# A two-layer hybrid decoder on one core: the order of two bank drains at the middle of a down unit, and where on-chip buffers begin

## The chip, the core and the metric

The kernel runs on one core of a Trainium2 chip. TensorE multiplies out of the on-chip memory (SBUF) into eight accumulation banks (PSUM), each 128 partitions by 512 float32 numbers; VectorE (DVE in the profile) and ScalarE (ACT) do the elementwise work and read the banks; SyncE (SP) issues the loads from HBM. The metric is the device time of one execution in microseconds. Three executions of the kernel before took 2243.55, 2243.8 and 2245.27 us, with a median of 2243.8 us.

## What is computed

Two layers on 256 tokens of width 2048, all in float32. Each layer has a mixing half (gated linear attention and stick-breaking attention side by side, one input and one output projection) and a squared-ReLU MLP with 8192 hidden columns. The change touches the end of the MLP in its order of work, and all of the kernel in where its buffers lie.

```python
D_MODEL, SEQ, DEPTH, D_FF = 2048, 256, 2, 4 * 2048

def hybrid_layer(x, ...):
    h = rms_norm(x, attn_norm)
    proj = h @ w_in                       # 2048 x 6160
    ...                                   # both head groups, from slices of proj
    x = x + mixed @ w_o                   # 2048 x 2048
    hm = rms_norm(x, mlp_norm)
    up = square(relu(hm @ w_up))          # 2048 x 8192
    return x + up @ w_down                # 8192 x 2048
```

## The kernel before

**Split products.** Every operand of the large products is held in the type `float32r` as two tiles, a high part and the remainder, called the low part, and each product is made of three: high times high, high times low, low times high. Weights come from HBM into a tile `raw`; ScalarE copies it to `whi` (the high part), VectorE subtracts to `wlo` (L358 and L360 for the projections, L990 and L991 for the down product). There are four buffers of `whi` and four of `wlo`, three of `raw`. Activations lie in 19 buffers of one size, `act`, high and low parts side by side.

**Three kinds of stage.** The projections are *units* (L365): weights move through TensorE, activations stay in the array as the stationary operand, 512 columns a product (L377 to L379). The up product and a part of the projections use the transposed form (`unit_t`, L411): activations move, weights are stationary, and a product of 512 columns (L424) is followed by one of 256 (L428). The down product (`mlp_down`, L961) is the third kind.

**A down unit.** The hidden columns are taken in four quarters a layer; for each quarter four `mlp_up` calls make 16 column blocks of `up`, and one down unit multiplies them with their 2048 rows of `w_down` and adds the result to the residual `xb`. So there are eight down units, four a layer. A unit goes through 16 `pairs` (L966), numbered `x`: the left 1024 output columns are x 0 to 7, the right 1024 are x 8 to 15; x takes 256 rows of `w_down`, one megabyte. For an even `j = x % 8`, and for j = 7, the block is multiplied plainly in two steps, `left` and `right` (L1071, L1076), 12 products each. For j = 1, 3 and 5 a scheme with sums of blocks saves products: seven block products instead of eight, in four steps (L1061). It needs sums of weight blocks, made by VectorE in `first` (L1037: the sums `ts`, then two more additions), and sums of activation blocks, made once during the up stage into tiles `sx` (L947). The first of the four steps is 6 products, the second 3, the third and fourth 6 each.

**The banks.** A half of a unit accumulates in eight banks, m1 to m8. When a half is done, its banks are added to `xb` by VectorE: m1, m5, m6, m7 after the last step of j = 5 (`drain`, L1049), m2 and m4 after `left` of j = 7 (`drain_left`, L1081), m3 and m8 after `right` of j = 7 (`drain_right`, L1087). The next half takes the same eight banks again (`new_banks`, L1006), so its first product into a bank waits for that bank's drain.

**The order.** In a down unit the instructions of TensorE, VectorE and ScalarE stand in the order in which the code records them. Each step has a part that prepares weights (`prepare`: splits and block sums, recorded at once) and a part with its products (`emit`, L1101: products, then the drain if the step has one). Steps go through a queue: when four are in it, the oldest is emitted. So the weights of a step are prepared three steps ahead of its products:

```python
for prepare, products, follow in steps(x):
    queue.append((x, products, prepare(), follow))
    if len(queue) >= LEAD:          # LEAD = 4
        emit(*queue.pop(0))
```

At the middle of a unit this gives the following order. Recording the preparation of x = 8 `right` emits x = 7 `left` with its drains of m2 and m4. Recording the first step of x = 9 (j = 1: the block sums) comes next, and only after it is x = 7 `right` emitted, with its drains of m3 and m8. "The second half" below means x 8 to 15, and "step 9a" to "step 9d" the four steps of x = 9.

**Buffers.** Pools are laid out in SBUF one after the other in the order in which they are opened (L67 to L72): constants, residual, activations, weights (`raw`, `whi`, `wlo`), temporaries, statistics, and then the pool of the attention or the MLP half (with `sx`, `ts`, `raw2`), which is reopened in turn.

Of the kernel before, what the change touches and what calls it, by code (L numbers as in the profile page):

```python
# [10 lines left out]
F32R = mybir.dt.float32r  # L11
# [5 lines left out]
P = 128  # L17
# [22 lines left out]
def trunk_kernel(  # L40
# [22 lines left out]
    def nm(s):  # L63
        uid[0] += 1
        return f"{s}_{uid[0]}"

    cpool = ctx.enter_context(tc.tile_pool(name="const", bufs=1))  # L67
    xpool = ctx.enter_context(tc.tile_pool(name="resid", bufs=1))
    apool = ctx.enter_context(tc.tile_pool(name="acts", bufs=19))
    wpool = ctx.enter_context(tc.tile_pool(name="weights", bufs=3))  # L70
    tpool = ctx.enter_context(tc.tile_pool(name="temps", bufs=2))
    spool = ctx.enter_context(tc.tile_pool(name="stats", bufs=6))  # L72

    pools = {}
    scopes = {}
# [44 lines left out]
    def f32(ap):  # L120
        return ap.bitcast(F32)
# [218 lines left out]
    def weight_parts(w2d, r0, c0, kt, width, fine=False, halves=1, order=lambda k: None):  # L340

        full = 2048 // kt
        raw = wpool.tile([P, kt, full], F32, tag="raw", name=nm("raw"))
        src = w2d[r0 : r0 + kt * P, c0 : c0 + width].rearrange("(k p) n -> p k n", p=P)
        step = 1 if fine else kt // halves
        for s in range(0, kt, step):
            nc.sync.dma_start(raw[:, s : s + step, :width], src[:, s : s + step, :])
        for s in range(2):
            hk = kt // 2
            hi = wpool.tile([P, hk, full], F32R, tag="whi", name=nm("whi"), bufs=4)  # L350
            lo = wpool.tile([P, hk, full], F32R, tag="wlo", name=nm("wlo"), bufs=4)
            step = 1 if fine else hk
            for q in range(0, hk, step):
                r = raw[:, s * hk + q : s * hk + q + step, :width]
                h = hi[:, q : q + step, :width]
                dep = order(s * hk + q)
                with tc.issue_after(dep) if dep else nullcontext():
                    newest["hi"] = nc.scalar.activation(h, r, AF.Copy).ins  # L358
                with tc.issue_after(st["first"]) if fine else nullcontext():
                    newest["lo"] = nc.vector.tensor_tensor(  # L360
                        lo[:, q : q + step, :width], r, f32(h), ALU.subtract
                    ).ins
            yield hi, lo

    def unit(op, w2d, row0, c0, width, groups=(0, 1, 2, 3), hooks={}, fine=0, split=False, order=lambda i, k: None):  # L365
# [17 lines left out]
        def prep(i):  # L383
            return weight_parts(
                w2d, row0 + 4 * groups[i] * P, c0, 4, width, fine=i < fine,
                halves=2 if fine else 1, order=lambda k: order(i, k),
            )
# [216 lines left out]
    for l in range(DEPTH):  # L604
# [356 lines left out]
        def mlp_down(q):  # L961
# [8 lines left out]
            def load(x):  # L970
                if x >= len(pairs):
                    return
                n2, j = pairs[x]
                if x % 5 < 2:
                    r = tmp("raw2", [P, 2, 1024], bufs=2)
                else:
                    r = wpool.tile([P, 2, 1024], F32, tag="raw", name=nm("raw"))
                raws[x] = r
                r0 = (q * KT + 2 * j) * P
                nc.sync.dma_start(  # L980
                    r,
                    w_down[l][r0 : r0 + 2 * P, n2 * 1024 : (n2 + 1) * 1024].rearrange(
                        "(k p) n -> p k n", p=P
                    ),
                )

            def parts(r, n=2):
                hi = wpool.tile([P, 2, 512], F32R, tag="whi", name=nm("whi"), bufs=4)
                lo = wpool.tile([P, 2, 512], F32R, tag="wlo", name=nm("wlo"), bufs=4)
                nc.scalar.activation(hi[:, :n], r, AF.Copy)  # L990
                nc.vector.tensor_tensor(lo[:, :n], r, f32(hi[:, :n]), ALU.subtract)  # L991
                return hi, lo
# [13 lines left out]
            def new_banks():  # L1006
                begun.clear()
                for m in (5, 1, 6, 7, 2, 4, 3, 8):
                    banks[m] = pools["m"].tile([P, 512], F32, tag=f"m{m}", name=nm(f"m{m}_"))

            def steps(x):
# [21 lines left out]
                if fast(j):  # L1033
# [3 lines left out]
                    def first():  # L1037
                        t13 = sums["t13"] = tmp("ts", [P, 2, 512], bufs=2)
                        t4 = sums["t4"] = tmp("t4", [P, 512], bufs=1)
                        b12 = r[:, 0, 512:]  # L1040
                        ends = r.rearrange("p k (c n) -> p (k c) n", c=2)[:, ::3, :]
                        nc.vector.tensor_tensor(  # L1042
                            t13, ends, b12.unsqueeze(1).to_broadcast([P, 2, 512]), ALU.add
                        )
                        add(b12, t13[:, 0, :], r[:, 1, 512:])
                        add(t4, b12, r[:, 1, :512])
                        return parts(r[:, 1, :].rearrange("p (c n) -> p c n", c=2))

                    def drain():  # L1049
# [11 lines left out]
                    return (  # L1061
                        (first, lambda w: (mm(2, blk(1, 0), w, 0, False), mm(3, ext(1), w, 1, False)), None),
                        (lambda: parts(sums["t4"].unsqueeze(1), 1), lambda w: mm(4, blk(1, 1), w, 0, False), None),
                        (lambda: parts(sums["t13"]),
                         lambda w: (mm(5, blk(0, 1), w, 0, lastf), mm(7, ext(2), w, 1, lastf)), None),
                        (lambda: parts(r[:, 0, :].rearrange("p (c n) -> p c n", c=2)),
# [32 lines left out]
            queue = []  # L1099

            def emit(x, products, w, follow):  # L1101
                if x % 8 == 0 and products.__name__ == "left":
                    new_banks()
                products(w)
                if follow:
                    follow()
# [2 lines left out]
                load(x)  # L1109
            for x in range(len(pairs)):  # L1110
                load(x + 4)
                for prepare, products, follow in steps(x):
                    queue.append((x, products, prepare(), follow))
                    if len(queue) >= LEAD:
                        emit(*queue.pop(0))
# [7 lines left out]
        for q in range(4):  # L1123
            if q:
                att_psum()
            for g in range(4):
                mlp_up(q, g)
            down_psum()
            with tc.manual_schedule(engines=MANUAL):
                mlp_down(q)  # L1130
# [40 lines left out]
```

## Time and profile before

| | before |
|---|---|
| median of three executions | 2243.8 us (2243.55 to 2245.27) |
| the profiled execution | 2244.34 us |
| its span, first to last instruction | 2242.6 us |
| TensorE busy | 2219.7 us |
| VectorE, ScalarE, GpSimd busy | 1628.6, 1171.0, 39.1 us |
| moved by DMA | 409.05 MB, 182 GB/s over the span |
| a down unit (the first, 508.5 to 594.2 us) | 85.7 us, TensorE busy 83.9, VectorE 75.5, ScalarE 45.3 |

The span is 1.7 us shorter than the profiled execution, which has its start and end around it. A matmul's duration in the profile runs to a modelled end and overlaps the next one's, so the time that a matmul costs is read as the distance from its start to the next one's start. "Idle" of an engine is counted from the end of its last instruction, and therefore is shorter than the gap between two starts. PE is TensorE, and PEld its weight load, which runs during the matmul before.

### The profile page before, as it was taken

The page shows a single profiled execution, that of the slowest core. Times are in us where ns is not written, and L with a number is a line of the kernel's source. Part 1 is how long each engine was busy: PE and PEld are TensorE (multiplying, and loading weights), DVE is VectorE, ACT ScalarE, POOL GpSimd, SP SyncE. Part 2 cuts the span into 40 slices and gives each one's busy share as a digit, 9 for nine tenths or more (in the row PEclk, how much of TensorE's full clock was granted, in tenths as well). Part 3 has the DMA queues.
Part 4 walks back from the last instruction along what each step waited for, and adds up shares of the span by engine and source line. Part 5 has one row for each costly group of instructions (what it writes and reads, how often), then busy time and mean ns, then how long its engine had stood idle before and what let it go on. Part 6 is the DMA issues. An engine that isn't in the chain of part 4 may idle for free.

```text
span 2242.6 us, 28461 instructions
## 1 busy us (share of the span) xinstructions
PE 2219.7 (99%) x11292; PEld 1858.6 (83%) x11292; DVE 1628.6 (73%) x2024; ACT 1171.0 (52%) x1499; POOL 39.1 (2%) x68
## 2 busy tenths in 40 slices
PE   9999999999999999999999999999999999999998
PEld 7988778887888888788788887888878878887887
DVE  5777565668868868867967775656787688688688
ACT  5555354555555455455555553555555545554553
POOL 0020000000000000000000200000000000000000
PEclk9999999999999999999999999999999999999999
DMA  6545446664665665565446544466656656656653
GB/s 228 189 158 162 151 144 232 187 188 169 214 186 188 201 188 187 190 195 179 169 135 204 171 151 150 154 225 184 188 183 203 187 178 207 188 181 210 185 180 127
DMA packets 250857, 409.05 MB, mean 182 GB/s; under 512 B 6650, under 2 KB 162882, under 8 KB 250724
## 3 DMA queue, kind: packets, MB, share of 16 engines
q1 hardware_dynamic: 250724, 407.24, 55.7%
q8 instruction: 88, 1.44, 0.3%
q14 instruction: 45, 0.37, 0.0%
HBM read 405.12 MB, written 2.10 MB: 182 GB/s over the span
## 4 chain that ended last, share of the span: by engine, by line
PE 91%; DVE 7%; issue 1%; ACT 1%; DMA 0%; POOL 0%; SPq 0%; POOLq 0%
PE acc L424 24%; PE acc L428 12%; PE acc L377 9%; PE acc L378 9%; PE acc L379 9%; DVE wlo L991 3%; DVE xb L1004 2%; DVE t L1004 1%; PE ps L294 1%; PE ps L847 1%; PE ps L859 1%; DVE ts L1042 0%; PE ps L806 0%; ACT whi L990 0%; PE ps L540 0%
## 5 line engine op out<-in xcount | busy, mean ns | idle before, releaser
L360 DVE TENSOR_TENSOR wlo<-raw,whi 128x1024 fp32r<-128x1024 f32 (+2 forms) x530 | 630.5, 1194 | 420.0 <-ACT whi L358 418.9
L358 ACT ACTIVATE whi<-raw 128x1024 fp32r<-128x1024 f32 (+2 forms) x530 | 545.3, 1032 | 643.9 <-PE acc L424 340.0
L424 PE MATMUL acc<-act,whi 128*128 128x512 f32 x2304 | 816.0, 399 | 0.0
L428 PE MATMUL acc<-act,wlo 128*128 128x256 f32 x2304 | 646.8, 281 | 0.0
L424 PEld LDWEIGHTS acc<-act,whi 128*128 128x128 f32 x2304 | 433.0, 188 | 106.5
L428 PEld LDWEIGHTS acc<-act,wlo 128*128 128x128 f32 x2304 | 435.2, 189 | 0.4
L377 PE MATMUL acc<-whi,act 128*128 128x512 f32 (+2 forms) x960 | 368.4, 384 | 0.5 <-ACT act L302 0.5
L378 PE MATMUL acc<-wlo,act 128*128 128x512 f32 (+2 forms) x960 | 361.9, 377 | 0.4 <-DVE wlo L360 0.4
L379 PE MATMUL acc<-whi,act 128*128 128x512 f32 (+2 forms) x960 | 361.6, 377 | 0.0
L991 DVE TENSOR_TENSOR wlo<-raw,whi 128x1024 fp32r<-128x1024 f32 x256 | 306.2, 1222 | 70.0 <-ACT whi L990 65.6
L990 ACT ACTIVATE whi<-raw 128x1024 fp32r<-128x1024 f32 x256 | 266.2, 1058 | 157.3 <-PE acc L424 29.0
L377 PEld LDWEIGHTS acc<-whi,act 128*128 128x128 f32 x960 | 180.9, 188 | 35.5 <-issue 4.1
L379 PEld LDWEIGHTS acc<-whi,act 128*128 128x128 f32 x960 | 180.5, 188 | 33.8 <-issue 0.7
L378 PEld LDWEIGHTS acc<-wlo,act 128*128 128x128 f32 x960 | 180.8, 188 | 32.0 <-DVE wlo L360 1.0
L990 ACT ACTIVATE whi<-t 128x512 fp32r<-128x512 f32 x48 | 30.4, 634 | 145.5 <-DVE t L1004 93.3
L991 DVE TENSOR_TENSOR wlo<-ts,whi 128x1024 fp32r<-128x1024 f32 x48 | 58.8, 1225 | 2.3 <-ACT whi L990 2.3
L1042 DVE TENSOR_TENSOR ts<-raw 128x1024 f32<-128x1024 f32 x48 | 58.5, 1218 | 0.0
L939 DVE TENSOR_TENSOR act<-t,act 128x512 fp32r<-128x512 f32 x64 | 44.1, 690 | 10.9 <-ACT act L938 10.9
L990 ACT ACTIVATE whi<-ts 128x1024 fp32r<-128x1024 f32 x48 | 50.2, 1045 | 0.0
L439 DVE TENSOR_TENSOR t<-acc,t 128x512 f32<-128x512 f32 x72 | 49.3, 684 | 0.0
L934 ACT ACTIVATE t<-t 128x512 f32<-128x512 f32 x64 | 39.6, 618 | 12.8 <-DVE t L930 12.8
L930 DVE SCALAR_TENSOR_TENSOR t<-t,row 128x512 f32<-128x512 f32 x64 | 44.3, 692 | 2.2
(1160 smaller groups left out, 2768.2 us busy)
## 6 DMA issues: line engine op xcount, KB each, us to landing
raw<-in_w_down_dram SPq DMA_DIRECT2D x128, 1024.0 KB, 5.3
raw<-in_w_up_dram SPq DMA_DIRECT2D x128, 1024.0 KB, 5.8
raw<-in_w_in_dram SPq DMA_DIRECT2D x84, 1024.0 KB, 5.1
raw<-in_w_o_dram SPq DMA_DIRECT2D x32, 1024.0 KB, 5.0
raw<-in_w_in_dram SPq DMA_DIRECT2D x14, 512.0 KB, 6.8
raw<-in_w_in_dram SPq DMA_DIRECT2D x8, 544.0 KB, 3.7
out_dram<-xb SPq DMA_DIRECT2D x8, 256.0 KB, 2.2
xb<-in_x_dram SPq DMA_DIRECT2D x3, 512.0 KB, 7.5
```

Of the source, the lines that this page charges most:

```text
L358: newest["hi"] = nc.scalar.activation(h, r, AF.Copy).ins
L360: newest["lo"] = nc.vector.tensor_tensor(lo[:, q : q + step, :width], r, f32(h), ALU.subtract).ins
L377: nc.tensor.matmul(o, xh[:, sl], whi[:, j, :width], start=first, stop=False)
L378: nc.tensor.matmul(o, xh[:, sl], wlo[:, j, :width], start=False, stop=False)
L379: st["mm"] = nc.tensor.matmul(o, xl[:, sl], whi[:, j, :width], start=False, stop=last).ins
L424: nc.tensor.matmul(acc[:, f, :], whi[:, j, sl], op.both(k), start=(k == 0), stop=False, skip_group_check=True,)
L428: nc.tensor.matmul(acc[:, f, T:], wlo[:, j, sl], xh, start=False, stop=(k == KT - 1), skip_group_check=True,)
L439: nc.vector.tensor_tensor(t, acc[:, :, :T], t, ALU.add)
L990: nc.scalar.activation(hi[:, :n], r, AF.Copy)
L991: nc.vector.tensor_tensor(lo[:, :n], r, f32(hi[:, :n]), ALU.subtract)
L1004: nc.vector.tensor_tensor(dst, a, b, ALU.subtract if sub else ALU.add)
L1042: nc.vector.tensor_tensor(t13, ends, b12.unsqueeze(1).to_broadcast([P, 2, 512]), ALU.add)
```

## The change

It has two parts.

**The drains.** Before the first step of x = 9 is prepared, steps of x below 8 that are still in the queue are emitted. In the queue stand then x = 7 `right`, x = 8 `left` and x = 8 `right`; the first is emitted, with its drains of m3 and m8. The queue is then one shorter, so that recording 9a emits nothing, and from 9b on all is as before.

**The bases.** The two split weights move from the pool `weights` to a pool of their own, `parts`, opened right behind the activations, and all other long-lived pools are laid out from the other end of SBUF (`side="right"`). The pool of the attention or MLP half, which has the activation sums `sx`, comes then right behind `parts`.

```diff
-    cpool = ctx.enter_context(tc.tile_pool(name="const", bufs=1))
-    xpool = ctx.enter_context(tc.tile_pool(name="resid", bufs=1))
+    cpool = ctx.enter_context(tc.tile_pool(name="const", bufs=1, side="right"))
+    xpool = ctx.enter_context(tc.tile_pool(name="resid", bufs=1, side="right"))
     apool = ctx.enter_context(tc.tile_pool(name="acts", bufs=19))
-    wpool = ctx.enter_context(tc.tile_pool(name="weights", bufs=3))
-    tpool = ctx.enter_context(tc.tile_pool(name="temps", bufs=2))
-    spool = ctx.enter_context(tc.tile_pool(name="stats", bufs=6))
+    ppool = ctx.enter_context(tc.tile_pool(name="parts", bufs=4))
+    wpool = ctx.enter_context(tc.tile_pool(name="weights", bufs=3, side="right"))
+    tpool = ctx.enter_context(tc.tile_pool(name="temps", bufs=2, side="right"))
+    spool = ctx.enter_context(tc.tile_pool(name="stats", bufs=6, side="right"))
...
-            hi = wpool.tile([P, hk, full], F32R, tag="whi", name=nm("whi"), bufs=4)
-            lo = wpool.tile([P, hk, full], F32R, tag="wlo", name=nm("wlo"), bufs=4)
+            hi = ppool.tile([P, hk, full], F32R, tag="whi", name=nm("whi"), bufs=4)
+            lo = ppool.tile([P, hk, full], F32R, tag="wlo", name=nm("wlo"), bufs=4)
...
-                hi = wpool.tile([P, 2, 512], F32R, tag="whi", name=nm("whi"), bufs=4)
-                lo = wpool.tile([P, 2, 512], F32R, tag="wlo", name=nm("wlo"), bufs=4)
+                hi = ppool.tile([P, 2, 512], F32R, tag="whi", name=nm("whi"), bufs=4)
+                lo = ppool.tile([P, 2, 512], F32R, tag="wlo", name=nm("wlo"), bufs=4)
...
-                for prepare, products, follow in steps(x):
+                for i, (prepare, products, follow) in enumerate(steps(x)):
+                    if x == 9 and i == 0:
+
+                        while queue[0][0] < 8:
+                            emit(*queue.pop(0))
                     queue.append((x, products, prepare(), follow))
                     if len(queue) >= LEAD:
                         emit(*queue.pop(0))
```

In the two built programs every engine has the same instructions; the order differs on VectorE alone, at one place in each of the eight down units. The rows that follow are VectorE's at that place in the first unit, before. A name is a tile and its number, `m3__795` is bank m3 of the left half, and `xb0`, `xb1` are the residual's column blocks.

```order
L991 TENSOR_TENSOR wlo_848_4694<-raw_817_4540,whi_847_4693 128x1024
L1004 TENSOR_TENSOR xb0_98<-m2__793_4420,xb0_98 128x512
L1004 TENSOR_TENSOR xb0_98<-m4__794_4421,xb0_98 128x512
L1042 TENSOR_TENSOR ts_850_4713<-raw_822_4559 128x1024
L1004 TENSOR_TENSOR raw_822_4559<-ts_850_4713,raw_822_4559 128x512
L1004 TENSOR_TENSOR t4_851_4714<-raw_822_4559 128x512
L991 TENSOR_TENSOR wlo_853_4719<-raw_822_4559,whi_852_4718 128x1024
L1004 TENSOR_TENSOR xb1_99<-m3__795_4422,xb1_99 128x512
L1004 TENSOR_TENSOR xb1_99<-m8__796_4423,xb1_99 128x512
L991 TENSOR_TENSOR wlo_855_4737<-t4_851_4714,whi_854_4736 128x512
```

The same place in the program of the change (its lines are one higher here, and tiles made after the pools have numbers three higher).

```order
L992 TENSOR_TENSOR wlo_848_4697<-raw_817_4543,whi_847_4696 128x1024
L1005 TENSOR_TENSOR xb0_101<-m2__793_4423,xb0_101 128x512
L1005 TENSOR_TENSOR xb0_101<-m4__794_4424,xb0_101 128x512
L1005 TENSOR_TENSOR xb1_102<-m3__795_4425,xb1_102 128x512
L1005 TENSOR_TENSOR xb1_102<-m8__796_4426,xb1_102 128x512
L1043 TENSOR_TENSOR ts_850_4730<-raw_822_4562 128x1024
L1005 TENSOR_TENSOR raw_822_4562<-ts_850_4730,raw_822_4562 128x512
L1005 TENSOR_TENSOR t4_851_4731<-raw_822_4562 128x512
L992 TENSOR_TENSOR wlo_853_4736<-raw_822_4562,whi_852_4735 128x1024
L992 TENSOR_TENSOR wlo_855_4740<-t4_851_4731,whi_854_4739 128x512
```

The drains of m3 and m8 have moved up past four instructions: the three of the block sums and the split of step 9a. Nothing else has moved.

TensorE's rows at the change from x = 8 `right` to step 9a, with the engines that a row waits for, show the one wait that is new. Before:

```order
L1000 MATMUL m8__863_4747<-wlo_848_4694,act_674_3698 128x512
L1001 MATMUL m8__863_4747<-whi_847_4693,act_674_3698 128x512
L998 MATMUL m2__860_4744<-whi_852_4718,act_689_3799 128x512 [waits Activation_49]
L1000 MATMUL m2__860_4744<-wlo_853_4719,act_689_3799 128x512
L1001 MATMUL m2__860_4744<-whi_852_4718,act_689_3799 128x512
```

And in the change:

```order
L1001 MATMUL m8__863_4750<-wlo_848_4697,act_674_3701 128x512
L1002 MATMUL m8__863_4750<-whi_847_4696,act_674_3701 128x512
L999 MATMUL m2__860_4747<-whi_852_4735,act_689_3802 128x512 [waits Activation_49]
L1001 MATMUL m2__860_4747<-wlo_853_4736,act_689_3802 128x512 [waits DVE_49]
L1002 MATMUL m2__860_4747<-whi_852_4735,act_689_3802 128x512
```

Before, the wait for the drain of m8 stood behind the split `wlo_853` on VectorE and covered it; in the change the second product of 9a has a wait for that split of its own.

The bases, in bytes from the start of a partition and modulo 1024, are these in the built programs:

| tile | before | modulo 1024 | change | modulo 1024 |
|---|---|---|---|---|
| `act` (19) | 38592 to 112320 | 704 | 16512 to 90240 | 128 |
| `whi` (4) | 140992 to 153280 | 704 | 94336 to 106624 | 128 |
| `wlo` (4) | 157376 to 169664 | 704 | 110720 to 123008 | 128 |
| `sx` (3) | 185152 to 191296 | 832 | 127104 to 133248 | 128 |
| `raw` (3) | 116416 to 132800 | 704 | 182688 to 199072 | 416 |
| `raw2` (2), `ts` (2), `t4` | 194368 to 218944 | 832 | 136320 to 160896 | 128 |
| `xb` (4) | 22208 to 34496 | 704 | 207264 to 219552 | 416 |
| `ident` | 16512 | 128 | 223648 | 416 |
| `t2` (4) | 173760 to 179904 | 704 | 171936 to 178080 | 928 |

## The prediction, made before the change was run

> **What bounds the kernel now.** I read the page's busy shares first, then the granted clock, then the chain that ended last.
>
> ```profile
> span 2242.6 us, 28461 instructions
> PE 2219.7 (99%) x11292; PEld 1858.6 (83%) x11292; DVE 1628.6 (73%) x2024; ACT 1171.0 (52%) x1499; POOL 39.1 (2%) x68
> PEclk9999999999999999999999999999999999999999
> PE 91%; DVE 7%; issue 1%; ACT 1%; DMA 0%; POOL 0%; SPq 0%; POOLq 0%
> ```
>
> TensorE is busy 99% of the span at the full granted clock, and 91% of the chain is its own. Time can therefore come from two places only: gaps in TensorE's sequence, and the distance between the starts of two matmuls. The 7% of VectorE in the chain say that some gaps wait for VectorE. The view of one source line (L998, the first of the three matmuls of a down product) says which:
>
> ```profile
> its engine sat idle before it (us, times) until:
>   ACT whi L990: 17.2, 8
>   DVE xb L1004: 14.1, 8
> ```
>
> Eight times, once in each down unit, TensorE sat idle before this line until an addition of a bank to the residual was done, 14.1 us in all. (The 17.2 us are the weight load of the same products, which stands behind the same wait; what it is put down to is a copy that merely ended at that time.) Idle is counted from a modelled end, so I price it by starts, in TensorE's timeline of the first unit:
>
> ```profile
> 545.73 0.39 PE L998 MATMUL m__793_4420<-whi,act 128*128 128x512 f32 x1
> ...
> 550.26 0.39 PE L1001 MATMUL m__796_4423<-whi,act 128*128 128x512 f32 x1
> ...
> 552.98 0.39 PE L1001 MATMUL m__861_4745<-whi,act 128*128 128x512 f32 x1
> 555.13 0.47 PE L998 MATMUL m__862_4746<-whi,act 128*128 128x512 f32 x1 [1.76 <-DVE xb L1004]
> 555.44 0.39 PE L1000 MATMUL m__862_4746<-wlo,act 128*128 128x512 f32 x1
> ```
>
> From 545.73 to 550.26 there are 20 products, 4.53 / 20 = 0.2265 us each: the undisturbed cost of a 512-column product. The one at 552.98 is followed by the next only 2.15 us later, 1.92 us too late, and that one's successor comes 0.31 us later, 0.08 too late. A stall costs **2.00 us**. It stands before the first product of x = 8 `right`, the first into bank m3 in the second half.
>
> **Part one: the drains.** Why it waits stands in VectorE's timeline of the same stretch:
>
> ```profile
> 549.38 0.68 DVE L1004 TENSOR_TENSOR xb<-m__793_4420,xb 128x512 f32<-128x512 f32 x1
> 549.98 0.68 DVE L1004 TENSOR_TENSOR xb<-m__794_4421,xb 128x512 f32<-128x512 f32 x1
> 550.58 1.22 DVE L1042 TENSOR_TENSOR ts<-raw 128x1024 f32<-128x1024 f32 x1
> 551.83 0.69 DVE L1004 TENSOR_TENSOR raw<-ts,raw 128x512 f32<-128x512 f32 x1
> 552.56 0.69 DVE L1004 TENSOR_TENSOR t<-raw 128x512 f32<-128x512 f32 x1
> 553.17 1.22 DVE L991 TENSOR_TENSOR wlo<-raw,whi 128x1024 fp32r<-128x1024 f32 x1
> 554.30 0.68 DVE L1004 TENSOR_TENSOR xb<-m__795_4422,xb 128x512 f32<-128x512 f32 x1
> 554.90 0.68 DVE L1004 TENSOR_TENSOR xb<-m__796_4423,xb 128x512 f32<-128x512 f32 x1
> 555.50 0.68 DVE L991 TENSOR_TENSOR wlo<-t,whi 128x512 fp32r<-128x512 f32 x1
> 556.10 1.22 DVE L991 TENSOR_TENSOR wlo<-ts,whi 128x1024 fp32r<-128x1024 f32 x1
> ```
>
> VectorE has no gap here. The drain of m3 (m__795) ends at 554.98 and TensorE starts at 555.13. The products into m8 end at 550.26 + 0.39 = 550.65, and those into m3 six products earlier, by 549.3; the drains stood in line behind four instructions. In the change they stand right behind the drain of m4. At the pace of 0.60 us of these additions, m3's runs from 550.58 to 551.26 and m8's from 551.18, after m8's last product, to 551.86. TensorE wants m3 at 552.98 + 0.23 = 553.21 and m8 six products later, so neither makes it wait. The stall goes whole, and x = 8 `right` ends its twelve products at 553.21 + 12 x 0.2265 = 555.93.
>
> What is late next: the four instructions passed by the drains start 1.20 us later each, `ts` at 551.78, then 553.03, 553.76, and the split of 9a at 554.37, ending at 555.59. It gets a wait of its own on TensorE: the second product of 9a, at 555.93 + 0.23 = 556.16. Cover 0.5 us, so I cost the move at nothing; with that cover gone, every further microsecond on VectorE would cost one per unit. ScalarE's copy of the block sum waits for the third of these instructions and comes with it:
>
> ```profile
> 553.36 0.63 ACT L990 ACTIVATE whi<-t 128x512 fp32r<-128x512 f32 x1 [4.33 <-PE m__861_4745 L1001]
> 553.90 1.04 ACT L990 ACTIVATE whi<-ts 128x1024 fp32r<-128x1024 f32 x1
> ```
>
> 553.36 becomes about 554.55, and the copy of `ts` about 555.10 to 556.15. The split for 9b may start after 555.5, as before; it is wanted at 555.93 + 6 x 0.23 + 0.23 = 557.5 and done by 556.2. The split of `ts` starts behind ScalarE's copy at 556.25 instead of 556.10, ends at 557.5, and is wanted for 9c at 555.93 + 9 x 0.23 + 0.23 = 558.2. From there the second half runs as the first does, which has the same steps and no stall. Nothing on SyncE's queue is passed, and loads do not tighten: the longest wait for weights from HBM in the list of waits is this one, and it is the only one of its group.
>
> ```profile
> ACT whi L358 <- DMA raw<-in_w_in_dram: 5.1, 1, 5.1
> ```
>
> So part one is 8 x 2.00 = **16.0 us**.
>
> **Part two: the bases.** In the profile of before there is one kind of large product whose operands are not at equal bases: those with activation sums `sx`, 128 bytes beside `whi` and `wlo` modulo 1024. Their starts, in steps 9a, 9c and 9d, each from the product of `act` ahead of them to the one behind:
>
> ```profile
> 558.39 0.40 PE L1001 MATMUL m__860_4744<-whi,act 128*128 128x512 f32 x1
> 558.62 0.40 PE L998 MATMUL m__862_4746<-whi,sx 128*128 128x512 f32 x1
> 558.86 0.40 PE L1000 MATMUL m__862_4746<-wlo,sx 128*128 128x512 f32 x1
> 559.09 0.40 PE L1001 MATMUL m__862_4746<-whi,sx 128*128 128x512 f32 x1
> 559.33 0.39 PE L998 MATMUL m__861_4745<-whi,act 128*128 128x512 f32 x1
> 560.48 0.40 PE L1001 MATMUL m__856_4740<-whi,act 128*128 128x512 f32 x1
> ...
> 561.42 0.39 PE L998 MATMUL m__857_4741<-whi,act 128*128 128x512 f32 x1
> 561.88 0.40 PE L1001 MATMUL m__857_4741<-whi,act 128*128 128x512 f32 x1
> ...
> 562.81 0.40 PE L998 MATMUL m__860_4744<-whi,act 128*128 128x512 f32 x1
> ```
>
> Four distances each: 0.94, 0.94 and 0.93 us, where four undisturbed ones are 0.906. That is 0.03 + 0.03 + 0.02 = 0.09 us for each x with sums, of which there are 6 x 8 = 48, **4.3 us** if all of it goes. The ends are 0 (the place is not why these products are slow) and 4.3; I take 4.3, since shape, type and moving operand are those of the `act` products beside them, and the place is what differs.
>
> [...]
>
> All other bases move too, and no row shows an operand at the new phases. For VectorE and ScalarE the nearest rows are the same split with all operands at one phase, and with the source 128 bytes off:
>
> ```profile
> L991 DVE TENSOR_TENSOR wlo<-raw,whi 128x1024 fp32r<-128x1024 f32 x256 | 306.2, 1222 | 70.0 <-ACT whi L990 65.6
> L991 DVE TENSOR_TENSOR wlo<-ts,whi 128x1024 fp32r<-128x1024 f32 x48 | 58.8, 1225 | 2.3 <-ACT whi L990 2.3
> ```
>
> 1222 and 1225 ns: nothing, and both engines have slack (73% and 52% busy). For TensorE the common base goes from 704 to 128 and stays common, so I take 0. The bounds are two rows. If every large product became as slow as one beside `sx`, 0.09 / 12 = 0.008 us on each of the some 10,000 large products among the 11292 matmuls, it would cost 80 us. If the transposed stages became as fast as the others, the gain comes from these rows (a group of the page; a window of an up stage, whose second number is TensorE's busy time with its count; two starts in a unit 256 columns wide, nine products apart):
>
> ```profile
> L424 PE MATMUL acc<-act,whi 128*128 128x512 f32 x2304 | 816.0, 399 | 0.0
> 594.30:684.80 90.50, 90.50 (x514) 78.41 (x513) 62.04 (x75) 46.33 (x56) 0.00 (x0) 1.00 0.64 198
> 78.97 0.28 PE L378 MATMUL acc<-wlo,act 128*128 128x256 f32 x1
> ...
> 80.04 0.28 PE L378 MATMUL acc<-wlo,act 128*128 128x256 f32 x1
> ```
>
> In an up stage a pair of a 512- and a 256-column product takes 90.50 / 257 = 0.352 us. In the unit form the two would take 0.2265 + 1.07 / 9 = 0.3455. 0.0065 us on 2304 pairs is 15 us. These bases were equal already, so equality alone has not given it.
>
> **The sum**: 16.0 + 4.3 = 20.3 us, from the profiled execution's 2244.3 to 2224.0. The median of the runs shown stands 0.5 us below that execution, so I predict **2223.5 us**.
>
> **The rivals.** (A) The drains help, the place of `sx` does not: its products stay at 0.235 us. [...] 2243.8 - 16.0 = 2227.8. (B) The stall comes back at 9a: the block sums, now behind two drains, are late for TensorE. Against it stands the cover of 0.5 us; for it, that VectorE has no gap from 549.38 on. If the chain were 1.2 us longer than reckoned (two more additions), 0.7 us a unit return, 6 us in all: 2223.5 + 6 = 2229.5. (C) The new common base also frees the transposed stages: 2223.5 - 15 = 2208. (D) **Slower than before**: TensorE's cost per product depends on where a base stands and not only on whether bases are equal, and 128 is a worse place than 704. It decides from 20.3 us / 10,000 products = 0.002 us a product on; at half of the slowness seen beside `sx`, 0.004, the time is 2223.5 + 40 = 2263. Only the `sx` rows show that TensorE minds a place at all. (E) That the change does not do what it says is ruled out for the drains by the order of the rows on VectorE.
>
> **How the numbers follow.** Forecast 0.47, A 0.25, B 0.08, C 0.07, D 0.06, and 0.07 for a smaller loss from the bases that leaves the time between 2231 and 2243. The range of eight in ten takes the forecast, A and B, with 1.5 us above B and, below, half of C, as the base's effect has no row: 2215 to 2231. A change of 0.2%, 4.5 us, is about what a measurement of this kernel tells from none. Faster by more than that: the forecast, A, B, C and most of the smaller losses, 0.92; within it 0.03; slower 0.05.
>
> **What would show it.** In the profile after, TensorE has no idle before the first product of x = 8 `right`; VectorE's two drains stand ahead of `ts`; a down unit takes 85.7 - 2.0 - 0.5 = 83.2 us. The three `sx` products of a step take 0.906 us from the `act` product ahead to the one behind (A: 0.94). An up stage stays at 90.5 us (C: 88.8; D: longer, as would all units be). A new idle before the second product of 9a, released by the split, would be B. The prediction is wrong if the up stages move, or if a down unit is not 2 us shorter.

## The result, and the profile after

The change takes **2219.4 us**, the median of 4 runs (2218.5 to 2219.7), against 2244.0 for the kernel before on the same chip (2243.6 to 2245.3): the ratio is 0.9889, with an interval of 0.9872 to 0.9906. That is 24.6 us less; forecast were 20.3.

These are the page's lines of the change that answer to those shown of before: the span, the busy shares, the granted clock, the chain that ended last by engine, and VectorE's group of splits in the down units (count, then busy us and mean ns, then the idle time before them).

```profile
span 2217.5 us, 28469 instructions
PE 2208.2 (100%) x11292; PEld 1857.2 (84%) x11292; DVE 1627.6 (73%) x2024; ACT 1170.7 (53%) x1499; POOL 39.1 (2%) x68
PEclk9999999999999999999999999999999999999999
PE 98%; DVE 1%; issue 0%; DMA 0%; ACT 0%; POOL 0%; SPq 0%; POOLq 0%
L992 DVE TENSOR_TENSOR wlo<-raw,whi 128x1024 fp32r<-128x1024 f32 x256 | 305.6, 1221 | 48.2 <-ACT whi L991 44.6
```

VectorE's part of the chain fell from 7% to 1%, and TensorE's rose to 98%: the waits for the drains are gone. The split itself takes as long as before (1221 ns, from 1222), although all its operands lie at other bases. VectorE's timeline at the middle of the first down unit, and TensorE's from the last product of x = 8 `left` on (lines are one higher than before), show it in place:

```profile
548.16 0.68 DVE L1005 TENSOR_TENSOR xb<-m__793_4423,xb 128x512 f32<-128x512 f32 x1
548.76 0.68 DVE L1005 TENSOR_TENSOR xb<-m__794_4424,xb 128x512 f32<-128x512 f32 x1
549.36 0.68 DVE L1005 TENSOR_TENSOR xb<-m__795_4425,xb 128x512 f32<-128x512 f32 x1
549.96 0.68 DVE L1005 TENSOR_TENSOR xb<-m__796_4426,xb 128x512 f32<-128x512 f32 x1
550.55 1.21 DVE L1043 TENSOR_TENSOR ts<-raw 128x1024 f32<-128x1024 f32 x1
...
553.14 1.22 DVE L992 TENSOR_TENSOR wlo<-raw,whi 128x1024 fp32r<-128x1024 f32 x1
```

```profile
551.65 0.39 PE L1002 MATMUL m__861_4748<-whi,act 128*128 128x512 f32 x1
551.87 0.39 PE L999 MATMUL m__862_4749<-whi,act 128*128 128x512 f32 x1
...
554.59 0.39 PE L999 MATMUL m__860_4747<-whi,act 128*128 128x512 f32 x1
554.82 0.39 PE L1001 MATMUL m__860_4747<-wlo,act 128*128 128x512 f32 x1
555.05 0.39 PE L1002 MATMUL m__860_4747<-whi,act 128*128 128x512 f32 x1
555.27 0.39 PE L999 MATMUL m__862_4749<-whi,sx 128*128 128x512 f32 x1
...
555.95 0.39 PE L999 MATMUL m__861_4748<-whi,act 128*128 128x512 f32 x1
```

The first product into m3 (m__862) follows its predecessor after 0.22 us; before, 2.15 us. The second product of 9a starts at 554.82, and the split that it waits for ended at 553.14 + 1.22 = 554.36: 0.46 us to spare where the prediction had reckoned 0.5. From 555.05, the last `act` product, over the three of `sx` to 555.95 are 0.90 us: the pace of undisturbed products, where before had 0.94.

The windows of the first layer's first up stage, first down unit and second up stage (from the start of its first product to that of the next stage; length, then TensorE's busy time and count, and so on) give the sizes. Before:

```profile
416.83:508.54 91.71, 91.64 (x523) 79.42 (x522) 62.96 (x82) 49.56 (x66) 0.59 (x2) 1.00 0.61 186
508.54:594.41 85.87, 84.11 (x368) 68.69 (x367) 75.66 (x85) 45.28 (x49) 0.00 (x0) 1.00 0.54 184
594.41:684.86 90.45, 90.45 (x514) 78.39 (x512) 61.99 (x74) 46.33 (x56) 0.00 (x0) 1.00 0.64 198
```

And in the change (here the down unit stands last):

```profile
417.49:507.66 90.17, 90.10 (x523) 78.73 (x522) 62.81 (x82) 49.52 (x66) 0.59 (x2) 1.00 0.61 189
590.63:681.07 90.44, 90.44 (x513) 78.47 (x512) 61.97 (x74) 46.32 (x56) 0.00 (x0) 1.00 0.64 199
507.66:590.63 82.97, 82.97 (x368) 68.70 (x367) 75.69 (x85) 45.26 (x49) 0.00 (x0) 1.00 0.56 190
```

A down unit went from 85.87 to 82.97 us. Over all eight the gain is 2.85 to 2.92 us each, 23.1 us in all. The first up stage of each of the two layers went from 91.71 to 90.17, which was not forecast: 3.1 us more. The other up stages are where they were. The spans differ by 25.1, so some 1 us was lost elsewhere: TensorE's first projection starts 0.3 us later, and some stages of the mixing half are longer, by up to 0.22 us.

### The profile page after: what moved, and what is told of

It reads as the page before. It is cut to its first block, busy times and chain, and to the rows that moved or that the text cites. A ratio compares the mean times of both kernels' runs of the same rounds, so it can differ in the third digit from the quotient of the medians.

```text
span 2217.5 us, 28469 instructions
## 1 busy us (share of the span) xinstructions
PE 2208.2 (100%) x11292; PEld 1857.2 (84%) x11292; DVE 1627.6 (73%) x2024; ACT 1170.7 (53%) x1499; POOL 39.1 (2%) x68
## 4 chain that ended last, share of the span: by engine, by line
PE 98%; DVE 1%; issue 0%; DMA 0%; ACT 0%; POOL 0%; SPq 0%; POOLq 0%
PE acc L425 24%; PE acc L429 12%; PE acc L378 9%; PE acc L379 9%; PE acc L380 9%; PE ps L295 1%; PE ps L848 1%; PE ps L860 1%; PE ps L807 0%; PE ps L541 0%; PE ps L487 0%; DVE wlo L361 0%; PE ps L576 0%; PE ps L505 0%; DMA raw<-in_w_in_dram 0%
## 5 line engine op out<-in xcount | busy, mean ns | idle before, releaser
L992 DVE TENSOR_TENSOR wlo<-raw,whi 128x1024 fp32r<-128x1024 f32 x256 | 305.6, 1221 | 48.2 <-ACT whi L991 44.6
```

## The experiments

Four questions were put: what each part is worth alone, whether the place of `sx` is why its products were slow, which distances count, and later, what happens behind the stall. The theory: a product whose stationary operand is not at the base of the moving one (modulo 1024, as the change has it) is slow, and slows some products behind it. The rivals: the region of memory counts and not the base; or the slowness beside `sx` is an aftermath of the stall.

### Each part alone: e1 and e2

e1 has the change's drains and the bases of before; its diff against the change is that of the pools alone (in part):

```
-    ppool = ctx.enter_context(tc.tile_pool(name="parts", bufs=4))
...
-            hi = ppool.tile([P, hk, full], F32R, tag="whi", name=nm("whi"), bufs=4)
+            hi = wpool.tile([P, hk, full], F32R, tag="whi", name=nm("whi"), bufs=4)
```

> The drains are moved as in the change; all bases are those of before, with the sums at 832 modulo 1024 and act, whi and wlo at 704. The theory that the place of the sums makes their products slow expects the eight stalls of 2.0 us to be gone (8 x 2.0 = 16 us, so 2228 us where before is 2244), sx products still 0.94 us for three and the distance to the one behind, a down unit of 83.6 us, and first up stages of a layer still at 91.6 us. The rival that the slowness beside the sums is an aftermath of the stall expects the sx products at 0.906 us too, a down unit of 82.8 us and 2221 us.

e2 has the change's bases and the drains of before:

```
-                for i, (prepare, products, follow) in enumerate(steps(x)):
-                    if x == 9 and i == 0:
-
-                        while queue[0][0] < 8:
-                            emit(*queue.pop(0))
+                for prepare, products, follow in steps(x):
```

> The bases are those of the change, the drains stand where they stood before. The theory of the place expects the stall before the first product of x = 8 right to stay at 2.0 us in each of the eight units, three sx products at 0.906 us, a down unit 85.67 - 0.87 = 84.8 us, and 2237 us (48 x 0.145 = 7 us below 2244), or 2234 us if the gain of 1.54 us in the first up stage of each layer comes from the bases as well. The rival that the slowness is an aftermath of the stall expects sx at 0.94 us and 2244 us.

e1 took 2228.3 us (2227.8 to 2228.5) where before took 2245.0, a ratio of 0.9925 (0.9912 to 0.9937). Its span is 2226.6, **16.0 us** under that of before, which is the forecast of the drains (the medians differ by 16.8). Its down units take 83.87 us, 2.0 less than before, and the `sx` products are as slow as before, 235 ns from start to start on average, without a stall. That ends the rival of the aftermath. The view of the tile `sx` in e1 (TensorE's rows of m3 in the first unit's second half: minimum, median and maximum ns, first and last start) and the same rows of the change:

```profile
L998 PE MATMUL m__862_4746<-whi,sx x3: 404/404/405, 556.7 to 577.4; 128*128 128x512 f32 x3
L1000 PE MATMUL m__862_4746<-wlo,sx x3: 395/396/396, 556.9 to 577.6; 128*128 128x512 f32 x3
L1001 PE MATMUL m__862_4746<-whi,sx x3: 397/398/398, 557.2 to 577.9; 128*128 128x512 f32 x3
```

```profile
L999 PE MATMUL m__862_4749<-whi,sx x3: 389/389/389, 555.3 to 575.7; 128*128 128x512 f32 x3
L1001 PE MATMUL m__862_4749<-wlo,sx x3: 389/389/389, 555.5 to 575.9; 128*128 128x512 f32 x3
L1002 PE MATMUL m__862_4749<-whi,sx x3: 389/389/389, 555.7 to 576.1; 128*128 128x512 f32 x3
```

e2 is the surprise: **2249.5 us** (2242.4 to 2251.3; ratio 1.0015, 1.0006 to 1.0024), slower than before, where 2237 was expected. Its `sx` products are at 226.7 ns from start to start, and in six of its units all is as expected: 85.1 us instead of 85.9. The seventh takes 86.7, and the starts of the last, which no stage follows, show as much. TensorE's timeline at the stall of the seventh unit, and windows of the same place (the column ahead of the last two is the granted clock):

```profile
2017.54 0.39 PE L1002 MATMUL m__2993_16780<-whi,act 128*128 128x512 f32 x1
2019.77 0.47 PE L999 MATMUL m__2994_16781<-whi,act 128*128 128x512 f32 x1 [1.84 <-DVE xb L1005]
2020.07 0.54 PE L1001 MATMUL m__2994_16781<-wlo,act 128*128 128x512 f32 x1
2020.41 0.63 PE L1002 MATMUL m__2994_16781<-whi,act 128*128 128x512 f32 x1
2020.84 0.63 PE L999 MATMUL m__2994_16781<-whi,act 128*128 128x512 f32 x1
...
2023.40 0.48 PE L999 MATMUL m__2995_16782<-whi,act 128*128 128x512 f32 x1
2023.71 0.40 PE L1001 MATMUL m__2995_16782<-wlo,act 128*128 128x512 f32 x1
```

```profile
2017.76:2019.77 2.01, 0.17 (x2) 0.04 (x1) 2.01 (x4) 1.58 (x2) 0.00 (x0) 1.00 0.75 300
2020.41:2023.40 2.99, 2.99 (x9) 2.31 (x7) 1.54 (x2) 0.00 (x0) 0.00 (x0) 0.50 0.00 0
```

From 2020.41 to 2023.40 seven products start 0.427 us apart at a granted clock of 0.50. The stretch lasts 3.4 us with its ends, and the unit is 1.6 longer than its neighbours. The stall is 2.00 us (2019.77 - 2017.54 - 0.23); before it was 1.92 in all eight units, and there is no such stretch in its profile. The three x with sums ahead of the stall no longer hold TensorE up; by an estimate from their 0.145 us each it comes to the drains 0.43 us earlier, VectorE by less, and the stall grew by 0.1 us. The mean clock of e2's executions lay between 0.995 and 0.998, that is at two to seven such stretches each (3.4 us at half clock take 1.7 / 2242 = 0.0008 off the mean). So the bases alone gain 0.78 us a unit and pay 1.6 us in some. Is the stall's length what calls it up, or the denser work around it? That is for e5 and e10.

### Is it the place? e3, e4, e6, e8, e12

All five are the change (e4: the kernel before) with unused bytes, by two lines whose number and position vary:

```
+    pad = ctx.enter_context(tc.tile_pool(name="pad", bufs=1))
+    pad_t = pad.tile([P, 32], F32, name="pad_t")
```

e3, e12 and e6 have 128, 64 and 256 bytes behind the `parts` pool, so that `sx` alone is off (with it the scratch tiles); e8 has 128 ahead of `act`, which moves all; e4 has 896 in the kernel before, ahead of `sx`.

> The change whole, but 128 unused bytes ahead of the sums: sx at 256 modulo 1024, act, whi and wlo at 128. If the base relative to the weights modulo 1024 makes the sx products slow, they are at 0.94 us for three again, with the products of step b and of the next left at 35 ns and more above theirs, 0.145 us for each x with sums, a down unit of 83.6 us, and 2219.4 + 7.0 = 2226.4 us. If the new region of memory (the sums now lie beside the weights, all other pools on the other side) is what freed them, 128 bytes change nothing: 0.906 us and 2219.4 us.

> The kernel before, with 896 unused bytes ahead of the sums: sx at 704 modulo 1024, equal to act, whi and wlo; drains, pools and sides as before. If equality modulo 1024 is what counts, the sx products take 0.906 us for three, a down unit 85.67 - 0.87 = 84.8 us, and the kernel 2244 - 7 = 2237 us, with the stall of 2.0 us kept. If the region or the common base 128 counts, sx stays at 0.94 us and the kernel at 2244 us.

> The change, with 256 unused bytes ahead of the sums: sx at 384 modulo 1024, act, whi and wlo at 128. At 512 bytes apart (the two halves of every act tile) the rows show no slowness, 226.7 ns a product; at 128 apart it was 0.145 us for each x with sums. If the slowness grows with the distance from the nearest multiple of 512, it is at least as large here: down units of 83.9 us or more, 2228 us or more. If only odd multiples of 128 matter, the sx products are at 226.7 ns, the down unit at 83.0 us and the kernel at 2219.5 us (2222.5 if the first up stages stay at 91.7 us).

> The change, with 128 unused bytes ahead of act: act, whi, wlo and sx all at 256 modulo 1024 instead of 128, equal as before. If only equality counts, down units stay at 83.0 us and the kernel at 2219.4 us, apart from the first up stage of each layer: 90.2 or 91.7 us, since a disturbance of 1 to 2 ns behind two small transposes picks there between pairs of 346.6 and of 353.3 ns. If the place of the common base counts, stages with equal bases move: units, down units or up stages by more than 0.2 us each.

> The change, with 64 unused bytes ahead of the sums: sx at 192 modulo 1024, act, whi and wlo at 128. 128 bytes off cost 0.87 us a down unit, 256 and 512 off nothing. If what counts is in which 128 bytes of each 256 the bases lie, sx at 192 lies with the others (128 to 255): down units of 83.0 us, 2219.5 to 2222.5 us. If any distance that is no multiple of 256 costs, the unit is between 83.0 and 83.9 us: half of the loss is 83.4 us and about 2223 to 2226 us.

| kernel | `sx` off by | a down unit, us | lost in it, ns | first up stages, us | time, us |
|---|---|---|---|---|---|
| change | 0 | 82.97 to 83.05 | 41 | 90.17, 90.17 | 2219.4 |
| e12 | 64 | 83.57 to 83.59 | 621 | 90.17, 91.71 | 2225.4 |
| e3 | 128 | 83.85 to 83.87 | 901 | 91.71, 91.71 | 2228.3 |
| e6 | 256 | 82.99 to 83.01 | 34 | 91.71, 91.71 | 2221.7 |
| e8 | 0, all at 256 | 82.98 to 83.05 | 55 | 91.71, 91.70 | 2222.0 |
| e1 | 128, bases of before | 83.87 to 83.90 | 910 | 91.71, 91.70 | 2228.3 |

The fourth column is the sum over a unit of what each distance between two starts, in whole ns, has above 226.67, as a mean of the eight units. The sizes of units and stages are from start to start; the unit that ends the program has no stage behind it and is left out.

128 unused bytes bring the whole slowness back (901 ns a unit, e1's is 910), and e3's time, less the 3.1 us of its first up stages, would be 2225.2 us, where 2226.4 were expected: the base it is, and not the region, since in e3 `sx` lies where it lies in the change but for 128 bytes. That the scratch tiles moved with it is not the cause either: in e7, below, they are equal to `sx` and to the weights, and the products of `act` are slow. Zero and 256 bytes are free, and so are 512: each `act` tile has halves 512 bytes apart, and rows of both are at 226.7 ns. At 64 it costs two thirds (621 ns of 901), more than the half that was put down as a middle case. So of the distances tried 0, 256 and 512 are free, and 64 and 128 cost. Another common base made no difference (e8: 55 ns lost in a unit, 41 in the change): its time differs from the change's by its first up stages. The view of `sx` in e12 and in e6, the same product as above:

```profile
L1001 PE MATMUL m__862_4753<-whi,sx x3: 398/398/398, 555.4 to 576.0; 128*128 128x512 f32 x3
```

```profile
L1001 PE MATMUL m__862_4753<-whi,sx x3: 389/389/389, 557.1 to 577.5; 128*128 128x512 f32 x3
```

e4, expected at 2237, took 2247.2 us (2244.7 to 2249.0). Equal bases alone do cure the `sx` products here too, with pools and region as before; but behind five of its eight stalls (2.00 to 2.02 us) stand the stretches of half clock seen in e2, and units with one take 86.7 to 86.8 us where those without take 85.1 (before: 85.9).

### What calls up the half clock? e5 and e10

e5 is the kernel before, bases and all, with a longer stall; e10 is e2 with a shorter one:

```
+                        if n2 and j == 1:
+                            add(t4[:, :8], b12[:, :8], b12[:, :8])
```

```
-                        add(t4, b12, r[:, 1, :512])
+                        if not (n2 and j == 1):
+                            add(t4, b12, r[:, 1, :512])
...
+                    def second():
+                        if n2 and j == 1:
+                            add(sums["t4"], r[:, 0, 512:], r[:, 1, :512])
+                        return parts(sums["t4"].unsqueeze(1), 1)
```

> The kernel before, with the sums' bases as they were (128 bytes off), and one addition of 8 elements (some 0.15 us) on VectorE ahead of the block sums of x = 9. It lengthens the stall before the first product of x = 8 right from 1.92 to about 2.07 us. In the bases-only kernel and in the one with 896 unused bytes the stall was 2.00 to 2.03 us and TensorE ran at a granted clock of 0.50 (427 ns a product) for 3.4 us behind it in 2 and in 5 of the eight units; in before, at 1.92 us, in none. The theory that the length of the stall decides expects such stretches here too, 1.7 us each in about three to eight units, a mean clock below 0.999 and 2244 + 1.2 + 5 to 13 = 2250 to 2259 us. The rival that undisturbed products (equal bases) are what calls them up expects none, clock 1.000 and 2245.5 us.

> The bases of the change, the drains where they were, and in x = 9 the third block sum (0.69 us) put behind the two drains: the stall before the first product of x = 8 right becomes 2.0 - 0.69 = 1.3 us. The theory that the stall's length calls up the half clock expects none of it: mean clock 1.000, every down unit 85.1 - 0.7 = 84.4 us, and the kernel 2244 - 7.0 - 8 x 0.69 = 2231.5 us. The rival that it is called up by undisturbed products around any stall expects stretches of 427 ns again, 1.7 us each, and 2235 to 2243 us.

e5, expected at 2250 to 2259, took 2253.0 us (2251.2 to 2253.8; ratio 1.0036, 1.0023 to 1.0049): the addition of 8 elements cost 8.3 us. It lengthened the stall by 0.07 us, to 1.99 (not to 2.07), which is 0.6 us in eight units; five of the eight then have a stretch of half clock, with `sx` as slow as ever. TensorE's timeline at the stall of the second unit:

```profile
730.36 0.39 PE L1001 MATMUL m__1108_6178<-whi,act 128*128 128x512 f32 x1
732.58 0.47 PE L998 MATMUL m__1109_6179<-whi,act 128*128 128x512 f32 x1 [1.83 <-DVE xb L1004]
...
733.74 0.63 PE L1000 MATMUL m__1109_6179<-wlo,act 128*128 128x512 f32 x1
734.17 0.63 PE L1001 MATMUL m__1109_6179<-whi,act 128*128 128x512 f32 x1
```

e10, with undisturbed products and stalls of 1.28 to 1.31 us, has none, and took 2230.6 us (2231.5 expected) with down units of 84.36 to 84.40. So in these runs the **length of the stall** decides, between 1.92 us (before: none of eight units) and 1.99 us (e5: five of eight): denser work around it is not needed. A stall of 1.92 us with all products undisturbed was not run.

Why in some units and not in all: the onset of a stretch can be estimated from the starts (the start of the first product at 427 ns, less twice what the product ahead has above its 230 ns). In e4 the five onsets are at 907.21, 1084.68, 1671.77, 1849.25 and 2026.78 us. From the first to the others are 51.99, 223.99, 275.99 and 328.00 times 3.4133 us: they lie on a fixed grid. In e5, on its grid (733.43, 910.89, 1675.48, 1853.16 and 2207.99 us), the five stalls with a stretch behind them lie whole between two grid points, and the three without reach over one, with 1.8 us ahead of it and 0.1 to 0.2 behind. In e4 and e2, stalls of which at most 1.85 us lie in one interval have none either. Three stalls (one in e4, two in e2) end within 0.1 us of a grid point and have none, though by this count 1.99 us and more of each lie in one interval; a product lasts 0.16 us longer than the next one's start (0.39 against 0.23), so the idle may lie a little later than the starts say, and these are at the edge.

The half clock that stands at the end of every program (in before from 2242.03 us on) lies on the grid of the onsets in e2, e4 and e5, and so gives the grid of before too: by it the stalls of its first, fourth and seventh unit lie whole between two points, 0.7 to 0.8 us behind one, and no half clock follows them. So 1.92 us was too short also where all of it lies in one interval, and 1.99 us of the 3.41 were enough in e5.

The grid also makes the stretches come in rows: a unit of 85.1 us and an up stage of 90.44 are 175.5 us, 51.4 of these intervals, but with a stretch they are 177.2, 51.9 of them, and the next stall falls at nearly the same place. In e4 five units in turn had one.

### The other products: e7, and e9 built on it

e7 puts 128 bytes between `act` and `whi`, so that `sx` is equal to the weights and every other large product is not. e9 is made from its result: the units stay equal, and only the transposed stages (`unit_t`, kt = 8) read their weights 128 bytes further on.

```
+    def split_tiles(k, n, at):
+        return [
+            ppool.tile([P, 1088], F32R, tag=s, name=nm(s), bufs=4)[
+                :, at : at + k * n
+            ].rearrange("p (k n) -> p k n", k=k)
+            for s in ("whi", "wlo")
+        ]
...
+            hi, lo = split_tiles(hk, full, 32 if kt == 8 else 0)
...
+                hi, lo = split_tiles(2, 512, 0)
```

> The change, with 128 unused bytes between act and whi: act at 128 modulo 1024, whi, wlo and sx at 256. The sx products now have equal bases and all others do not. If unequal bases slow whatever product stands beside them, sx is at 226.7 ns and the act products of the down units at 0.94 us for four; at 6 to 14 ns for each of the about 270 act products of a down unit the unit becomes 1.6 to 3.8 us longer than 83.0, the other unit stages by the same share, and the kernel 2219 + 20 to 80 us. If sums are special (their region, the way they are written), act products stay at 226.7 ns and the kernel within 3 us of 2219.4 us.

> The change, with the split weights of the transposed (up) stages alone 128 bytes further: act and the units' and down units' whi, wlo and sx at equal bases, the up stages' weights 128 bytes (and multiples of 256) off. With act 128 off everywhere an up stage took 89.87 us where 90.44 is the rule, and the first one of a layer 91.22 us, while units and down units lost. If the same holds here, the six later up stages gain 0.57 us each, 3.4 us, the two first ones take 91.22 us (0.49 less than the usual 91.71, 1.05 more than the 90.17 of the change's profile), units and down units stay as in the change, and the kernel takes 2219.4 - 3.4 + 2.1 = 2218.1 us. If the gain in the up stages came from something else that was moved there (the sums' or the scratch tiles' place), they stay at 90.44 us and the kernel at 2219.4 to 2222.5 us.

> The change once more. Its profile had the first up stage of each layer at 90.17 us where every other kernel with an up stage of equal bases had 91.70 to 91.71. If that belongs to the program, it comes again and the times lie at 2218.5 to 2219.7 us. If it is drawn anew in each execution, some executions take 2219.4 + 1.5 or + 3.1 = 2221 to 2222.5 us and the profile shows 91.7 us in one or both.

e7 took 2244.7 us (2244.4 to 2245.4), as much as the kernel before: 25 us lost by 128 bytes. A down unit is 85.0 us, 2.0 above the change, with the loss turned round: in the steps of x = 2 and 4, which have `act` alone, 5 to 6 ns a product. The `sx` products, now at equal bases but behind disturbed ones, average 230 ns. The run of unit stages ahead of a layer's first up stage went from 119.06 to 121.78. But its up stages became shorter, 89.87 from 90.44 us, the second window here of e7 being the down unit:

```profile
599.82:689.69 89.87, 89.87 (x514) 78.76 (x513) 61.84 (x74) 46.30 (x56) 0.00 (x0) 1.00 0.65 198
514.82:599.82 85.00, 85.00 (x369) 68.96 (x368) 75.83 (x85) 45.30 (x49) 0.00 (x0) 1.00 0.54 187
```

e9 takes the one without the other; its second up stage, first down unit and first up stage:

```profile
591.45:681.32 89.87, 89.87 (x513) 78.76 (x512) 61.90 (x74) 46.31 (x56) 0.00 (x0) 1.00 0.66 199
508.44:591.45 83.01, 83.01 (x369) 68.70 (x367) 75.65 (x85) 45.24 (x49) 0.00 (x0) 1.00 0.56 190
417.20:508.44 91.24, 91.18 (x523) 79.82 (x522) 62.89 (x82) 49.53 (x66) 0.58 (x2) 1.00 0.62 186
```

It took **2217.0 us** (2218.1 expected; 2216.9 to 2217.5; ratio to before 0.9877, 0.9862 to 0.9892), where the change on the same chip (e11) took 2219.2 (2218.5 to 2219.9): the fastest version here, by 2 us, with 2.1 us given back in the two first up stages. Of the 2.4 us between the spans of e11 and e9 the up stages make 1.3; another 0.8 lie ahead of the first projection, whose start differs by 0.7 us between two runs of the change itself, and the rest lies in the mixing half, whose transposed stages the edit moves too.

e11 had its two first up stages at 90.17 us again, and so had e10; e2, e3, e6 and e8 had 91.70 to 91.71, and e12 one of each. In all of them the stage begins alike, and in the change and e2, which have the same bases and the same program up to there, the starts of TensorE are the same within 1 or 2 ns up to two small transposes some 9 us into the stage. From there on pairs of a 512- and a 256-column product follow each other at 346.7 ns in the change, for 80 us, and at 353.4 in e2 (over the same 100 pairs). What picks the pace was not found; it repeats with the program more than it changes between executions, and it is not the bases alone. One of e6's four executions took 2219.0 us where the others took 2221.6 to 2222.5; that is what the faster pace in both stages would give, but this execution has no profile.

## Why the prediction came out as it did

- **The drains** were right in mechanism and size: 8 x 2.00 = 16.0 us by the starts of one unit, 16.0 us between the spans of before and e1. That the split of 9a would be the next to be late, and not be late, held as well.
- **The bases** were right in mechanism, and the term was mis-sized. The step "0.03 + 0.03 + 0.02 = 0.09 us for each x with sums" counts from the `act` product ahead of the three `sx` products to the one behind. By the starts in whole ns, an x with sums loses 35 ns in step a, 11 in b, 35 in c, 33 in d, and the `left` step behind it 31 more: 145 ns, not 90. The 42 of steps b and `left` stand in products of `act` alone; the disturbed sequence took some more products to settle. 48 x 0.145 = 7.0 us where 4.3 were forecast, and e1 and the change differ by just that in their down units (83.87 against 82.97 to 83.05). The forecast of 83.2 us for a unit hides the mistake, because it starts from a window of 85.7 us; from start to start the unit of before took 85.87.
- **"An up stage stays at 90.5 us"** held for six of eight. The first of each layer lost 1.54 us, 3.1 in all, by a pace that the prediction did not know of. By its own words it is wrong there, and for its time these 3.1 us are luck. Rival C, which priced such a gain, met the pace (346.7 ns a pair, where it reckoned 345.5) but not the cause: the later up stages have the same bases and did not move, and e2, e6 and e8 have equal bases without it.
- The sum: 16.0 + 7.0 + 3.1 - 1.0 lost elsewhere = 25.1 us between the spans, against 20.3. So 2.7 of the 4.8 us that are missing were in a term that the profile of before did hold, and 2.1 in what it could not show.
- Rival A fell with e1 and e3, B with the 0.46 us of cover, D with e8, where another common base cost nothing. Its bound of 80 us for "all products as slow as one beside `sx`" was measured in e7 at 25: an `act` product alone loses 5 to 6 ns and not 8, and the transposed stages gain.
- What the sum took for granted is that its two terms add up. They do in this order only: the bases on top of the drains gain 9.1 us of span (2226.6 to 2217.5), and without the drains they lose 4.5 at the median. Had the change been the bases alone, the forecast by the same working would have been 2239.5, and 2249.5 the result.

## What to carry to other kernels

Where TensorE is the bound, read its distances from start to start for each pair of operands, over the products behind a slow one too; a few ns on one kind of product can be the base of one operand against the other (5 to 14 ns at 128 bytes here, e1 and e3), and a few unused bytes try it out. A stall had a second price here, paid behind it, where it was long enough to bring the clock down: the bases alone gained 0.78 us a unit, lengthened the stall from 1.92 to 2.00 us, and the kernel took 2249.5 us where before took 2245.0 (e2). So remove the stall first.

## What the runs showed of the hardware that was not expected

- A product of 512 columns in a down unit took 226.7 ns from start to start where the bases of its two operands are 0, 256 or 512 bytes apart modulo 1024 (the change, e6, e8), and more at the two other distances tried: 5 to 14 ns for the `sx` products at 128 bytes off (e1, e3), 3 to 9 at 64 (e12), 5 to 6 on average where all products are 128 off (e7). Some products of `act` behind it were slower too: 42 of the 145 ns that an x with sums loses in before. Transposed pairs of 512 and 256 columns, with `act` moving, went the other way: 90.44 us a stage at equal bases, 89.87 at 128 bytes off (e7, e9).
- Stalls of TensorE of 1.99 to 2.03 us that lay whole between two points of a fixed grid of 3.413 us were followed by 3.4 us at half clock (e2, e4, e5), but for three that ended within 0.1 us of a point; those of 1.92 us (before) and of 1.28 to 1.31 us (e10) were not.
- Pairs of a 512- and a 256-column product ran at 346.7 ns in the change and at 353.4 in e2, with the same bases, over the same 100 pairs of a first up stage; in the change they stayed at it for 80 us.
